# Block boundaries on all tokens at once: two chunks project the unnormed input and are scaled afterwards

## The chip, the cores and the metric

The kernel runs on one core of a Trainium2 chip. The time is device microseconds of one execution of the whole program, inputs in device memory at its start and the output there at its end. A profiled execution also gives a trace: every instruction of TensorE (PE, and PEld for its weight loads), VectorE (DVE), ScalarE (ACT), GpSimd (POOL) and the DMA queues, of which SyncE's (SP) issues nearly all loads.

## What is computed

Two layers on one sequence of 512 tokens with 1024 features, float32. Each layer is a token mixer and a gated MLP, and each of the four sub-layers starts with a norm that is modulated by a conditioning vector:

```python
mod = silu(c) @ ada_w[i] + ada_b[i]
sh1, sc1, g1, sh2, sc2, g2 = split(mod, 6)
h = rms_norm(x, norm_mix[i]) * (1.0 + sc1) + sh1
x = x + g1 * mixer(h)           # layer 0: stick-breaking attention, layer 1: sparse attention with an index
h = rms_norm(x, norm_ffn[i]) * (1.0 + sc2) + sh2
x = x + g2 * conv_ffn(h)        # up-projection, causal conv of width 3, silu(gate) * value, down-projection
```

`rms_norm(x, g)` is `x * rsqrt(mean(x*x) + 1e-6) * g`, with one mean per token. So for one token with the factor r, `h = r * (s * x) + sh`, where s has a value per feature, and for a weight matrix W: `W^T h = r * (W^T (s * x)) + W^T sh`. The right side is what the change uses.

## The kernel before

Everything is kept transposed: features on the 128 partitions, tokens along the row. x is eight tiles of 128 x 512 (`x0` to `x7`), and so is the normed input h. Float32 products are made of three matmuls on a rounded high part and the rest, the low part: high x high, low x high, high x low (`mm3`, lines 249 to 251). Weights come as chunks of 128 x 1024 through six `raw` buffers; ScalarE makes the high part (`whi`, line 209), VectorE the low part (`wlo`, line 217), four buffers of each. A chunk's high part can be made only when PE is done with the chunk four before it. The order of the chunks is a fixed list (`split_order`), and the program says by `split_hi` and `split_lo` where in the queues the next one is split.

A **boundary** is the stretch between two sub-layers: the last output projection (tiles `pt_l`), the residual `x = x + gate * pt_l` (`add_to_x`, line 371, VectorE), the mean of squares (`pt_norm`, `pt_part` on PE with a matrix of ones), the norm factor (a ScalarE seed and three VectorE steps, lines 333 to 335), the normed input (`u` on VectorE, its high part `hhi` on ScalarE, its low part `hlo` on VectorE), and the first four chunks of the next sub-layer (`pt_first`). There are three: attention to MLP of layer 0, MLP to the sparse attention of layer 1, and that to the MLP of layer 1. Each is written by `boundary` in two halves of 256 tokens: the second half's projection covers the first half's norm, the first half of `pt_first` covers the second half's norm, and `second_half` ends the four chunks and hands each result to its consumer. All matmuls of a boundary are thus 256 columns wide. In program order each engine has one queue; the order in the code is the order in the queue, and a scheduler does not reorder inside this part.

Behind a boundary the MLP evacuates each chunk by `evac_up`: ScalarE writes `y` from PSUM (line 999), VectorE adds two shifted products (lines 1000 and 1001), and for a pair `mix` makes silu (ScalarE), the product, and its high (`acthi`, line 233) and low part. Projections use three PSUM banks (`mm`). Behind the second boundary the consumers are the index keys (`kd`, `kl`), the index weights (`kw`) and the query tiles (`qs`, made by `qi_evac`); then come index scores `z`, eight heads of three matmul pairs, between whose heads steps of the next projections are put (`fill`, `drain`).

The modulation is made on VectorE, one dot (line 258) per 128 columns: 24 in the first attention, one or two per head, 56 in the first MLP, one behind each chunk (`ada_steps`).

Of the kernel before, what the change touches and what calls it, by code (L numbers as in the profile page):

```python
# [9 lines left out]
F32 = mybir.dt.float32  # L10
# [9 lines left out]
S = 512  # L20
# [40 lines left out]
def chunk_order():  # L61
# [19 lines left out]
    keys += [("uv",)]  # L81
    return {k: i for i, k in enumerate(keys)}
# [38 lines left out]
def kernel_body(ctx, tc, xT, wst, cst, smalls, crow, ccol, relb, onehot, outT):  # L121
# [28 lines left out]
    sfac = cpool.tile([P, KT], F32, name="sfac")  # L150

# [61 lines left out]
    def split_lo(new=split_tile, engine=dve):  # L213
        while pend_lo:
            k, n, raw, hi = pend_lo.pop(0)
            lo = new("wlo")
            engine.tensor_sub(lo[:, :n], raw[:, :n], hi[:, :n].bitcast(F32))  # L217
            ready[k] = (hi, lo)
# [34 lines left out]
    ada_jobs = [(l, g, f) for l in range(DEPTH) for g in (1, 0, 2, 4, 3, 5) for f in range(KT)][2 * KT:]  # L253
    ada_state = {"i": 0, "cap": 3 * KT}
# [5 lines left out]
    def ada_steps(n):  # L260
        for _ in range(n):
            if ada_state["i"] >= ada_state["cap"]:
                return
            l, g, f = ada_jobs[ada_state["i"]]
            ada_state["i"] += 1
            ada_dot(mod[l][:, g * KT + f:g * KT + f + 1], chunk_raw(("ada", l, g, f)))
# [4 lines left out]
    def ada_until(n):  # L271
        ada_steps(n - ada_state["i"])
# [11 lines left out]
    def square(f, hf):  # L284
        t = npool.tile([P, H2], F32, name="sqt", bufs=5)
        act.activation(t, x[f][:, halves[hf]], AF.Square)
        return t

    def square_add(f, t):
        if f == 0:  # L290
            a = sqs["acc"] = npool.tile([P, H2], F32, name="sqa")
            dve.tensor_copy(a, t)
        else:
            dve.tensor_add(sqs["acc"], sqs["acc"], t)

    def sum_squares(t, start, stop):
        if start:
            sqs["pt"] = ptile([P, H2], "pt_norm", "z")
        pe.matmul(sqs["pt"], lhsT=ones_mean, rhs=t, start=start, stop=stop)

    def quarter_squares(ts, first):

        if first:
            sqs["parts"] = ptile([P, H2], "pt_part", "z")
        for i, t in enumerate(ts):
            pe.matmul(sqs["parts"][32 * i:32 * i + 32], lhsT=ones_mean[:, :32], rhs=t, start=first, stop=not first)

    def quarters_out():
        t = sqs["sum"] = npool.tile([P, H2], F32, name="sqt", bufs=5)
        act.activation(t, sqs["parts"], AF.Copy, scale=D / 32)  # L310
# [1391 lines left out]
```

## Time and profile before

| | |
|---|---|
| median of three runs | 1275.79 us (1274.8 to 1276.78) |
| the profiled execution | 1274.89 us, span 1272.8 us |
| PE busy | 1258.4 us, 99% |
| VectorE, ScalarE busy | 909.3 us (71%), 601.4 us (47%) |
| granted PE clock | 1.00 |
| first, second, third boundary, from the first `pt_l` matmul to the first matmul behind the `pt_first` group | 50.56, 50.94, 50.85 us |

The span is what the trace covers. The page's lists give busy time per engine; a timeline row gives the start, the duration, engine, line and operation, output and inputs, and in brackets the idle time before it with what ended it. A matmul's duration is longer than its distance to the next one, since matmuls are pipelined. A row of a window gives its ends and length, then the busy time (and instructions) of PE, PEld, VectorE, ScalarE and GpSimd, the granted clock, the DMA engines' share and GB/s.

### The profile page before, as it was taken

What the parts mean: (1) busy time and instruction counts of PE and PEld (TensorE: products, weight loads), DVE (VectorE), ACT (ScalarE), POOL (GpSimd) and SP (SyncE); (2) the same over time, 40 slices, a digit from 0 to 9 for tenths busy, and PEclk for the clock granted to TensorE, in tenths of its full rate; (3) what the DMA queues carried; (4) which work ended last, traced back from release to release, by engine and by line L of the source; (5) the groups of instructions that cost most, each with busy time, mean ns of one, the idle gap of its engine ahead of it and who ended that gap; (6) DMA issues with size and microseconds to landing.
All of it is one profiled execution on the core that took longest, in us unless ns stands there. A gap on an engine that the chain in (4) does not pass through costs nothing.

```text
span 1272.8 us, 17764 instructions
## 1 busy us (share of the span) xinstructions
PE 1258.4 (99%) x6774; PEld 1050.5 (83%) x6774; DVE 909.3 (71%) x1543; ACT 601.4 (47%) x1067; POOL 123.9 (10%) x129
## 2 busy tenths in 40 slices
PE   8999999999999999999999999999999999999998
PEld 6988787898888888888897788778988888888887
DVE  5889998778777877885778876567766456456653
ACT  6477666454323323442456357775553334334430
POOL 0000000000000000000002357773000000000000
PEclk9999999999999999999999999999999999999999
DMA  9644434323575575655222211142222322423231
GB/s 372 227 132 134 144 128 139 120 67 128 199 254 185 178 241 191 191 182 157 85 67 67 100 50 51 53 147 68 83 91 74 121 91 75 128 84 100 75 91 67
DMA packets 49893, 163.41 MB, mean 128 GB/s; under 512 B 5728, under 2 KB 7008, under 8 KB 49808
## 3 DMA queue, kind: packets, MB, share of 16 engines
q1 hardware_dynamic: 49376, 161.49, 38.7%
q8 instruction: 53, 0.87, 0.3%
q10 hardware_dynamic: 432, 0.79, 0.2%
q14 instruction: 32, 0.26, 0.1%
HBM read 160.12 MB, written 2.14 MB: 127 GB/s over the span
## 4 chain that ended last, share of the span: by engine, by line
PE 89%; DVE 6%; ACT 2%; DMA 2%; issue 1%; POOL 1%; SPq 0%; DVEq 0%; ACTq 0%
PE pt_u L249 11%; PE pt_u L250 11%; PE pt_u L251 11%; PE pt_d L250 5%; PE pt_d L249 5%; PE pt_d L251 5%; PE pt_first L249 2%; PE pt_first L251 2%; PE pt_first L250 2%; PE pt_q L249 2%; PE pt_q L251 2%; PE pt_q L250 2%; PE pt_l L250 2%; PE pt_l L249 2%; PE pt_l L251 2%; PE pt_qk L249 1%
## 5 line engine op out<-in xcount | busy, mean ns | idle before, releaser
L209 ACT ACTIVATE whi<-raw 128x1024 fp32r<-128x1024 f32 (+1 forms) x206 | 205.3, 1003 | 116.3 <-PE pt_d L251 88.2
L249 PE MATMUL pt_u<-hhi,whi 128*128 128x512 f32 x640 | 249.2, 389 | 0.0
L250 PE MATMUL pt_u<-hhi,wlo 128*128 128x512 f32 x640 | 249.0, 389 | 0.0
L251 PE MATMUL pt_u<-hlo,whi 128*128 128x512 f32 x640 | 249.0, 389 | 0.0
L217 DVE TENSOR_TENSOR wlo<-raw,whi 128x1024 fp32r<-128x1024 f32 (+1 forms) x186 | 214.0, 1152 | 14.1 <-ACT whi L209 13.2
L999 ACT ACTIVATE y<-pt_u,sm 128x512 f32<-128x512 f32 x80 | 62.2, 777 | 188.0 <-PE pt_u L251 188.0
L249 PEld LDWEIGHTS pt_u<-hhi,whi 128*128 128x128 f32 x640 | 120.1, 188 | 26.0 <-issue 1.1
L251 PEld LDWEIGHTS pt_u<-hlo,whi 128*128 128x128 f32 x640 | 120.1, 188 | 24.9
L250 PEld LDWEIGHTS pt_u<-hhi,wlo 128*128 128x128 f32 x640 | 120.2, 188 | 24.7
L1000 DVE SCALAR_TENSOR_TENSOR y<-pt_u,sm,y 128x511 f32<-128x511 f32 x80 | 59.9, 749 | 96.6 <-ACT y L999 96.4
L249 PE MATMUL pt_d<-acthi,whi 128*128 128x512 f32 x288 | 112.0, 389 | 0.0
L250 PE MATMUL pt_d<-acthi,wlo 128*128 128x512 f32 x288 | 112.0, 389 | 0.0
L251 PE MATMUL pt_d<-actlo,whi 128*128 128x512 f32 x288 | 112.0, 389 | 0.0
L258 DVE SCALAR_TENSOR_TENSOR raw<-raw,cond 128x1024 f32<-128x1024 f32 x88 | 106.6, 1217 | 4.7 <-DMA raw<-wst 4.7
L371 DVE SCALAR_TENSOR_TENSOR x<-pt_d,mod,x 128x512 f32<-128x512 f32 x48 | 36.0, 750 | 72.8 <-PE pt_d L251 72.8
L233 ACT ACTIVATE acthi<-y 128x512 fp32r<-128x512 f32 x44 | 27.8, 632 | 105.8 <-DVE y L1018 105.8
L249 PE MATMUL pt_first<-hhi,whi 128*128 128x256 f32 (+1 forms) x224 | 68.3, 305 | 0.0
L250 PE MATMUL pt_first<-hhi,wlo 128*128 128x256 f32 (+1 forms) x224 | 67.1, 299 | 0.8 <-DVE wlo L217 0.8
L251 PE MATMUL pt_first<-hlo,whi 128*128 128x256 f32 (+1 forms) x224 | 66.9, 299 | 0.0
L249 PEld LDWEIGHTS pt_d<-acthi,whi 128*128 128x128 f32 x288 | 54.1, 188 | 11.3
L251 PEld LDWEIGHTS pt_d<-actlo,whi 128*128 128x128 f32 x288 | 54.1, 188 | 11.2
L250 PEld LDWEIGHTS pt_d<-acthi,wlo 128*128 128x128 f32 x288 | 54.1, 188 | 11.2
(253 smaller groups left out, 2655.6 us busy)
## 6 DMA issues: line engine op xcount, KB each, us to landing
raw<-wst SPq DMA_DIRECT2D x250, 512.0 KB, 3.7
raw<-wst SPq DMA_DIRECT2D x48, 384.0 KB, 3.0
th<-rb SPq DMA_DIRECT2D x16, 256.0 KB, 3.4
ada<-wst SPq DMA_DIRECT2D x4, 512.0 KB, 6.3
outT<-x SPq DMA_DIRECT2D x6, 256.0 KB, 2.0
x<-xT SPq DMA_DIRECT2D x5, 256.0 KB, 5.1
x<-xT ACTq DMA_DIRECT2D x3, 256.0 KB, 4.0
cond<-crow SPq DMA_DIRECT2D x1, 512.0 KB, 10.7
```

The costliest lines, as they stand in the source:

```text
L209: act.activation(hi[:, :n], raw[:, :n], AF.Copy)
L217: engine.tensor_sub(lo[:, :n], raw[:, :n], hi[:, :n].bitcast(F32))
L233: act.activation(hi, src, AF.Copy)
L249: pe.matmul(out, lhsT=whi, rhs=ahi, start=start, stop=False)
L250: pe.matmul(out, lhsT=wlo, rhs=ahi, start=False, stop=False)
L251: pe.matmul(out, lhsT=whi, rhs=alo, start=False, stop=stop)
L258: dve.scalar_tensor_tensor(raw, raw, 1.0, cond, op0=OP.mult, op1=OP.mult, accum_out=dst)
L371: dve.scalar_tensor_tensor(x[f][:, c], pt, mod[l][:, g * KT + f:g * KT + f + 1], x[f][:, c], op0=OP.mult, op1=OP.add)
L999: act.activation(y, pt, AF.Identity, scale=cw[2], bias=sm[:, b + S_CB + c:b + S_CB + c + 1])
L1000: dve.scalar_tensor_tensor(y[:, 1:], pt[:, :S - 1], cw[1], y[:, 1:], op0=OP.mult, op1=OP.add)
```

## The change

`boundary` works on all 512 tokens. It projects all of `pt_l` with full-width matmuls, 512 columns. Right behind each residual tile ScalarE makes its square and the rounded `x * s` (`xs`, tiles that `place` takes from buffers free at that moment), VectorE the low part of `x * s`. The first two of the four chunks project `xs`, without the norm. Meanwhile squares are added up on VectorE and PE makes one 512-wide sum behind the third k of these two chunks; then come the norm factor and the normed input, 512 wide, and the other two chunks on it. The first two results are multiplied by the token's factor (`rescale`, VectorE) and get `W^T sh` as a bias per row (`bcol`, ScalarE). `second_half` is gone: consumers take the four results at the end.

`bcol` is made by VectorE dots of a new weight layout (`bt` chunks) with the shift as a row. The shift is a column of `mod`; it is written to device memory and read back as a row on all partitions, four jobs later. This job stands in the list of modulation dots: one in the first attention, two in the first MLP. The list's first groups are reordered, two heads of the attention take a job more, and the first MLP starts its dots one pair of chunks later.

In the sparse attention `kl`'s second half is copied by ScalarE, five fill steps of the fourth query chunk stand ahead of the index scores, and value tiles are 512 wide instead of two of 256.

```diff
-    ada_jobs = [(l, g, f) for l in range(DEPTH) for g in (1, 0, 2, 4, 3, 5) for f in range(KT)][2 * KT:]
-    ada_state = {"i": 0, "cap": 3 * KT}
+    ada_jobs = [(0, g, f) for g in (2, 3, 4) for f in range(KT)]
+    for at, what in ((19, "col"), (23, "row")):
+        ada_jobs.insert(at, ("bias", 0, what))
...
+            nc.sync.dma_start(shifts[n], mod[l][:, g * KT:(g + 1) * KT])
+        else:
+            ov = shifts[n][0:1, 0:1]
+            row = raws.tile([P, D], F32, name="shrow", tag="raw")
+            nc.sync.dma_start(row, bass.AP(tensor=ov.tensor, offset=ov.offset, ap=[[0, P], [1, D]]))
+            for i in range(2):
+                raw = chunk_raw(("bt", n, i))
+                dve.scalar_tensor_tensor(raw, raw, 1.0, row, op0=OP.mult, op1=OP.mult,
+                                         accum_out=bcol[:, 2 * n + i:2 * n + i + 1])
...
-        ops0 = norm_ops(nl, sh, 0)
-        pend = []
-        for m in range(KT):
-            if m == 1:
-                sum_squares(sqs["acc"], True, False)
-                sum_squares(prev, False, True)
-                norm_seed(0)
-            if m == 5:
-                quarter_squares(pend[:4], True)
-            pend.append(out_tile(1, m))
...
+        goals = {0: last[2], 1: last[3], 2: first[0], 4: first[1], 6: first[2]}
...
+            add_to_x(l, gate, m, begun.pop(m))
+            square(m)
+            xs[m] = place(m)
+            act.activation(xs[m][0], x[m], AF.Copy, scale=sfac[:, m:m + 1])
+            if m > 1:
+                square_add(m - 1)
+            if m == KT - 1:
+                square_add(m)
+            if m:
+                scaled_lo(m - 1)
+            split_lo()
+            if m in goals:
+                while pos["i"] <= order.index(goals[m]):
+                    split_hi()
...
+        def rescale(i):
+
+            v = npool.tile([P, S], F32, name="v", tag="sqt", bufs=2)
+            dve.tensor_mul(v, pts[i], rstd["r"])
+            act.activation(v, v, AF.Identity, bias=bcol[:, 2 * n + i:2 * n + i + 1])
+            vs.append(v)
...
+            first_steps((0, 1), xs, k)
+            if k == 2:
+                sum_squares()
+                norm_seed()
+                norm_newton()
+        cs += [chunk(k, 0) for k in first[2:]]
+        for k in range(KT + 1):
+            if k < KT:
+                norm_hi(nl, sh, k)
+            if k:
+                norm_lo(nl, sh, k - 1)
+                first_steps((2, 3), hs, k - 1)
+            if k in (4, 6):
+                split_hi()
+            if k == 6:
+                rescale(0)
+        split_lo(n=1)
+        rescale(1)
+        return pts, vs
...
-        for i in range(4):
-            project(pts[i][:, halves[1]], cs[i], hcur["h"], halves[1])
-            if i in ahead:
-                split_hi()
-            finish(i, pts[i])
-            split_lo()
...
-                    if l == 0:
+                    if l == 0 and j >= 3:
                         ada_steps(1)
...
-                    dve.tensor_sub(kl[64:], pt[64:], kd[64:].bitcast(F32))
...
+                act.activation(kl[64:], kl[64:], AF.Copy)
...
+                ptq = ptile([P, S], "pt_qi", "mm")
+                fill = project_steps(ptq, chunk(("qi", 3), 0))
+                drain(fill, 5)
```

Three places in the queues. VectorE in the first boundary's last projection; `pt_l` is the projected tile, `sqa` the sum of squares, `xkd` and `xkz` low parts of the scaled x, `nt` and `ln` the norm factor. Before:

```order
L371 SCALAR_TENSOR_TENSOR x_94<-pt_l,mod_87,x_94 128x256
L294 TENSOR_TENSOR sqa<-sqa,sqt 128x256
L371 SCALAR_TENSOR_TENSOR x_95<-pt_l,mod_87,x_95 128x256
L294 TENSOR_TENSOR sqa<-sqa,sqt 128x256
L371 SCALAR_TENSOR_TENSOR x_96<-pt_l,mod_87,x_96 128x256
L294 TENSOR_TENSOR sqa<-sqa,sqt 128x256
```

Now:

```order
L371 SCALAR_TENSOR_TENSOR x_97<-pt_l,mod_87,x_97 128x512
L322 TENSOR_TENSOR sqa<-sqa,sqt 128x512
L409 SCALAR_TENSOR_TENSOR xkd_2663<-x_96,sfac,xkd_2662 128x512
L371 SCALAR_TENSOR_TENSOR x_98<-pt_l,mod_87,x_98 128x512
L322 TENSOR_TENSOR sqa<-sqa,sqt 128x512 x2
L409 SCALAR_TENSOR_TENSOR xkz_2686<-x_97,sfac,xkz_2685 128x512
L220 TENSOR_TENSOR wlo<-raw,whi 128x1024
L409 SCALAR_TENSOR_TENSOR xkz_2711<-x_98,sfac,xkz_2710 128x512
L220 TENSOR_TENSOR wlo<-raw,whi 128x1024
L348 TENSOR_TENSOR nt<-ln 128x512
```

A tile has three operations instead of two, of double width, and two weights' low parts stand ahead of the norm factor.

PE in the first two chunks of the first boundary, as it is now:

```order
L254 MATMUL pt_first<-xolo,whi 128x512
L252 MATMUL pt_first<-xohi,whi 128x512
L253 MATMUL pt_first<-xohi,wlo 128x512
L254 MATMUL pt_first<-xolo,whi 128x512
L326 MATMUL pt_norm<-sqa,ones_mean 128x512
L252 MATMUL pt_first<-xohi,whi 128x512
```

The one sum of squares stands between the third and the fourth k; before, there were three sums and two groups of quarter sums per boundary.

ScalarE behind the first boundary; `v` is a rescaled chunk, `y` a chunk's first conv product, `acthi` the high part of the gated product, `whi` a weight's. Before:

```order
L209 ACTIVATE whi<-raw 128x1024
L999 ACTIVATE y_3035<-pt_first,sm 128x512
L386 ACT_TABLE_LOAD
L386 ACTIVATE ecols<-ecols 128x1
L209 ACTIVATE whi<-raw 128x1024
L999 ACTIVATE y_3070<-pt_first,sm 128x512
L1015 ACTIVATE y_3035<-y_3035 128x512
L233 ACTIVATE acthi<-y_3070 128x512
L209 ACTIVATE whi<-raw 128x1024
```

Now:

```order
L455 ACTIVATE v<-v,bcol 128x512
L386 ACT_TABLE_LOAD
L386 ACTIVATE ecols<-ecols 128x1
L991 ACTIVATE y_2886<-v,sm 128x512
L991 ACTIVATE y_2892<-v,sm 128x512
L1007 ACTIVATE y_2886<-y_2886 128x512
L236 ACTIVATE acthi<-y_2892 128x512
L211 ACTIVATE whi<-raw 128x1024
L991 ACTIVATE y_2906<-pt_first,sm 128x512
```

The first `y` now stands behind both rescaled chunks and the table load, and the high part of the next MLP chunk behind `acthi`.

More of the change, by code (lines that the diff above doesn't have):

```diff
@@ L81, in chunk_order @@
     keys += [("uv",)]
+    keys += [("bt", n, i) for n in range(3) for i in range(2)]
     return {k: i for i, k in enumerate(keys)}
@@ L260, in ada_steps @@
     def ada_steps(n):
-        for _ in range(n):
-            if ada_state["i"] >= ada_state["cap"]:
-                return
+        while n and ada_state["i"] < ada_state["cap"]:
             l, g, f = ada_jobs[ada_state["i"]]
             ada_state["i"] += 1
+            if l == "bias":
+                bias_job(g, f)
+                n -= f == "row"
+                continue
+            n -= 1
             ada_dot(mod[l][:, g * KT + f:g * KT + f + 1], chunk_raw(("ada", l, g, f)))
@@ L282, in kernel_body, with square, square_add, sum_squares @@
     sqs = {}
[L284 to L310, printed above, removed]
+    def square(f):
+        t = npool.tile([P, S], F32, name="sqa", tag="u", bufs=3) if f == 0 else \
+            npool.tile([P, S], F32, name="sqt", bufs=2)
+        act.activation(t, x[f], AF.Square)
+        sqs[f] = t
+    def square_add(f):
+        dve.tensor_add(sqs[0], sqs[0], sqs.pop(f))
+    def sum_squares():
+        sqs["pt"] = ptile([P, S], "pt_norm", "z")
+        pe.matmul(sqs["pt"], lhsT=ones_mean, rhs=sqs.pop(0), start=True, stop=True)
     hcur = {}
@@ L386, in warm, with boundary @@
         act.activation(spare, eps_c, func)
-    def boundary(last, O, l, gate, nxt, first):
+    def boundary(n, last, O, l, gate, nxt, first, place):
         cks = [chunk(k, 0) for k in last[:2]]
-        unsplit = lambda: pos["i"] <= order.index(last[3])
         nl, gcol, sh, sc = nxt
@@ L1324, in dsa_layer @@
                 O = []
[L1325 to L1327 removed]
+                uvc = [npool.tile([P, S], F32, name="uvc", tag="sqt", bufs=2) for i in range(2)]
+                for i in range(2):
+                    nc.sync.dma_start(uvc[i], wst[CH["uv",], :, i * S:(i + 1) * S])
                 heads = {}
@@ L1584, in dsa_layer, with place @@
                         follow(engine)
-                first = boundary([("do", 1, m) for m in range(4)], O[4:], l, 2, (l, S_NF, 3, 4), up_first(l))
+                def place(f):
+                    return [pp.tile([P, S], F32R, name="x" + t, tag=t, bufs=QRING) for t in ("qh", "ql")]
+                first = boundary(2, [("do", 1, m) for m in range(4)], O[4:], l, 2, (l, S_NF, 3, 4), up_first(l), place)
         return first, man
```

239 lines of the change are left out of this document (106 added, 133 removed).

## Prediction

> **What bounds the kernel now.** I read the page's first part, then its chain that ended last, then the busy time of each engine by stage, with the three boundaries as windows of their own, and last the timelines inside them.
>
> ```profile
> PE 1258.4 (99%) x6774; PEld 1050.5 (83%) x6774; DVE 909.3 (71%) x1543; ACT 601.4 (47%) x1067; POOL 123.9 (10%) x129
> PE 89%; DVE 6%; ACT 2%; DMA 2%; issue 1%; POOL 1%; SPq 0%; DVEq 0%; ACTq 0%
> 239.96:290.52 50.56, 49.59 (x408) 47.84 (x407) 36.86 (x76) 28.32 (x52) 0.00 (x0) 1.00 0.23 74
> 607.79:658.73 50.94, 49.90 (x407) 47.95 (x406) 37.55 (x78) 27.85 (x52) 1.75 (x6) 1.00 0.25 80
> 880.80:931.65 50.85, 49.91 (x408) 47.96 (x407) 39.20 (x78) 28.35 (x52) 2.15 (x1) 1.00 0.26 84
> ```
>
> TensorE (PE) is the bound: 99% of the span, 89% of the chain, at granted clock 1.00. A window row gives the length, then busy time of PE, PEld, DVE, ACT, POOL. The three windows are the boundaries, each from its first `pt_l` matmul to the first matmul behind its `pt_first` group: 50.56, 50.94 and 50.85 us. PE idles 1 us in each, VectorE 12 to 14 us, ScalarE 22 us. Only PE's instructions and its waits can move the time, but a busy PE is not one at its best rate; that is read from start to start:
>
> ```profile
> 271.80 0.28 PE L249 MATMUL pt_first<-hhi,whi 128*128 128x256 f32 x1
> 271.92 0.28 PE L250 MATMUL pt_first<-hhi,wlo 128*128 128x256 f32 x1
> ...
> 300.07 0.39 PE L249 MATMUL pt_u<-hhi,whi 128*128 128x512 f32 x1
> ...
> 300.75 0.39 PE L249 MATMUL pt_u<-hhi,whi 128*128 128x512 f32 x1
> 253.12 0.86 PE pt_norm L299 x4
> ```
>
> Half-width matmuls start every 0.120 us, full-width ones every 0.227 us (three in 0.68). So two halves cost 0.240.
>
> **PE's own work.** Each boundary has 384 half-width matmuls (96 products twice in `pt_l`, 96 twice in `pt_first`): 384 x 0.120 = 46.1 us. What is left of 50.56 is 4.5 us: the sums of squares in four pieces, and 1 us of waiting for the last squares. After the change there are 192 full-width ones, 192 x 0.2265 = 43.5, and one 512-wide sum, two passes, which I put at what four half-width passes take, 0.86. That is 44.4 us. Saved: 6.2, 6.5 and 6.5 us, 19.2 together, if nobody makes PE wait.
>
> The Trainium skill, "TensorE: Matmul & The Clock Gate", section "Back-to-back issue gap", speaks against most of the merging: a warm matmul costs its columns at 2.4 GHz plus 2.5 ns, so joining two saves 2.5 ns, an estimate of 0.5 us per boundary instead of 2.5. The trace disagrees: the pair above costs 13 ns more than the whole, so the measured spacing stands.
>
> **VectorE inside a boundary.** It now does all tokens' scaling twice: once unnormed for two chunks, once normed for two. Rates when it is queued:
>
> ```profile
> 222.69 0.69 DVE L927 TENSOR_TENSOR olo<-av,ohi 128x512 fp32r<-128x512 f32 x1
> 223.29 1.41 DVE L371 SCALAR_TENSOR_TENSOR x<-pt_o,mod,x 128x512 f32<-128x512 f32 x2
> 224.61 0.42 DVE L880 TENSOR_TENSOR_SCAN mz<-mz,diag 128x128 f32<-128x128 f32 x1
> 283.84 0.75 DVE L1000 SCALAR_TENSOR_TENSOR y<-pt_first,sm,y 128x511 f32<-128x511 f32 x1 [3.81 <-ACT y L999]
> 284.63 0.75 DVE L1001 SCALAR_TENSOR_TENSOR y<-pt_first,sm,y 128x510 f32<-128x510 f32 x1
> 285.29 1.21 DVE L217 TENSOR_TENSOR wlo<-raw,whi 128x1024 fp32r<-128x1024 f32 x1
> 259.06 1.23 DVE L217 TENSOR_TENSOR wlo<-raw,whi 128x1024 fp32r<-128x1024 f32 x1 [0.28 <-ACT whi L209]
> 260.20 0.48 DVE L342 SCALAR_TENSOR_TENSOR u<-ln,sfac,x 128x256 f32<-128x256 f32 x1
> 687.69 0.59 ACT L1091 ACTIVATE qh<-pt_q 128x512 fp32r<-128x512 f32 x1
> 688.17 0.60 ACT L1092 ACTIVATE q2g<-pt_q 128x512 f32<-128x512 f32 x1
> 268.19 1.04 ACT L209 ACTIVATE whi<-raw 128x1024 fp32r<-128x1024 f32 x1
> 269.14 0.36 ACT L310 ACTIVATE sqt<-pt_part 128x256 f32<-128x256 f32 x1
> ```
>
> From start to start: a 512-wide TENSOR_TENSOR 0.60, a 512-wide SCALAR_TENSOR_TENSOR 0.66 (0.79 when the next needs its result), a weight's low part 1.14, a 512-wide ACT copy 0.48, a weight's high part 0.95. The `pt_l` stage gives VectorE per tile `add_to_x` 0.66, the square's add 0.60 and the scaled input's low part 0.66, so 1.92, against 12 x 0.2265 = 2.72 us of PE. Three or four weights' low parts (five or six at the second and third boundary, whose last two chunks are not split yet) add 1.14 each. Counted from the first `pt_l` matmul, tile 0 is there at 4.9 (21 matmuls; the first two tiles interleave). Walking the queue in its printed order I get x7 at 22, the last add at 24.2, against PE's sum of squares at 21.7 + 18 x 0.2265 = 25.8: no wait, with 1.6 us to spare (1.2 at the other two). The low parts of tile 7 and of the fourth chunk end at 27.7; then come Newton's three steps, to 30.0. From there each k takes two 0.66 operations, 1.32, against 1.36 for PE's six matmuls: the first normed low part is ready at 32.4, PE wants it at 34, the last at 42.3 against 43.5. So PE never waits inside, by a margin of about 1 us; its bounds are 0 and the price in the last rival. Nearer to the boundary's end PE's spacing is a little wider in the trace:
>
> ```profile
> 290.52 0.40 PE L249 MATMUL pt_u<-hhi,whi 128*128 128x512 f32 x1
> ...
> 291.22 0.40 PE L249 MATMUL pt_u<-hhi,whi 128*128 128x512 f32 x1
> ```
>
> 0.233 instead of 0.227. I take 0.3 us per boundary for it (0 to 1.2, as if all 192 ran so): 0.9 in all.
>
> **What is late next: the first MLP chunks (boundaries one and three).** Before, the four chunks' results came 2.9 us apart (24 x 0.120) and were evacuated between. Now all four end almost together, with VectorE and ScalarE behind.
>
> ```profile
> 283.82 1.28 ACT L386 ACT_TABLE_LOAD   x1
> 285.12 0.20 ACT L386 ACTIVATE ecols<-ecols 128x1 f32<-128x1 f32 x1
> ...
> 290.82 1.43 ACT L999 ACTIVATE y<-pt_first,sm 128x512 f32<-128x512 f32 x2
> ```
>
> Low part of chunk `up 2,0` to 43.4, second rescale `v` to 43.9, its bias on ScalarE to 44.7, then table load and warm-up, 1.4, to 46.1, `y` 0.67 (two in 1.43), the two conv steps to 48.3, low part `up 2,1` to 49.5 (PE wants it at 50.1: in time), the second conv to 51, multiply 51.7, `acthi` 52.3. Only behind that, in ScalarE's queue, stands the high part of `up 3,0`, to 53.3; then `y` of the third chunk 54, its conv 55.4, and only then, in VectorE's queue, the low part, to 56.7. PE reaches that chunk at 44.4 + 48 x 0.2265 = 55.3 and wants the low part with its second matmul: 1.2 to 1.5 us of waiting, partly for the PSUM bank that the conv empties. `up 3,1` follows by the same round trip, 0.8 us late. From `up 4` on VectorE has 4.7 us less to do per pair of chunks than PE and the delay is gone. So 2.3 us at the first boundary, 2.7 at the third (two low parts more): 5.0. Bounds: 0 and 8.
>
> The Trainium skill, "ScalarE: Activation LUTs", section "What ACT_TABLE_LOAD costs", has 1.28 us plus a drain of 1.38. By it the chain would be 1.4 us longer at each of the two, and the forecast 2.8 us higher. The rows show the next ACT instruction 0.02 us behind the load, on an engine that had just ended its work; I keep 1.3.
>
> **The second boundary ends in the index scores.**
>
> ```profile
> 658.73:682.57 23.84, 23.66 (x117) 19.71 (x116) 19.34 (x32) 14.69 (x29) 0.00 (x0) 1.00 0.15 45
> 667.87 0.28 PE L1252 MATMUL z<-kd,qs 128*128 128x256 f32 x1
> ...
> 663.58 1.39 DVE L1174 TENSOR_TENSOR qs<-pt_first,qs 64x512 fp32r<-64x512 f32 x2 [0.26 <-ACT qs L1170]
> 665.00 2.07 DVE L1257 SCALAR_TENSOR_TENSOR work<-rl,wT,work 128x256 f32<-128x256 f32 x4
> ```
>
> Before, `kd`, `kl` and two query tiles were made while PE still projected; now the second rescaled chunk is ready at 44.9 and all follows: two `kd` copies, `kl`, its copy, two query copies, a low part, to 48.9. PE is covered by five of the eight fill steps, 15 x 0.23 = 3.5, and four transposes: 44.4 to 48.2. It waits 0.7. But those five steps are then missing between the scores of heads 0 to 2, where VectorE has two query pairs, a weight's low part and `wT` first (to 52.1) and then 1.6 us per head plus 1.4 for the next query pair: to 58.3. With two PSUM banks and three `rl` buffers PE can be about 0.7 ahead of that, so head 3 starts at 57.6. Before, it started at 667.87 - 607.79 = 60.1. Of 6.5 us gained 2.5 are left; 4.0 are lost (bounds 0 and 6.5: later heads have their fill as before).
>
> **Elsewhere.** Two modulation dots more (the shift row's) in the attention, where VectorE is the second bound, and a broadcast row with its two weight chunks through the six `raw` buffers; four more in the first MLP.
>
> ```profile
> 100.00:239.00 139.00, 138.68 (x823) 112.54 (x824) 127.89 (x194) 89.79 (x190) 0.00 (x0) 1.00 0.42 139
> 340.00:605.00 265.00, 265.00 (x1171) 219.43 (x1170) 200.09 (x282) 92.53 (x121) 0.00 (x0) 1.00 0.62 199
> L258 DVE SCALAR_TENSOR_TENSOR raw<-raw,cond 128x1024 f32<-128x1024 f32 x88 | 106.6, 1217 | 4.7 <-DMA raw<-wst 4.7
> ```
>
> 1.2 us each. The attention has 11 idle VectorE microseconds in 139, the MLP 65 in 265: four dots there cost nothing (0 to 5 if the cover were gone). The attention's two I put at 0.3 (0 to 2.4). The row's DMA stands on SP's queue behind the column's, written four jobs earlier, some 25 us at that stage's pace; SP should find it landed; if not, the weight loads queued behind it on SP wait, and PE for those. The boundaries load the same chunks as before. The `vals` copy as one instruction and the second table of values in two loads take a little off ScalarE: nothing on the path.
>
> **Sum.** 19.2 - 0.9 - 5.0 - 4.0 - 0.3 = 9.0 us. The profiled execution took 1274.89, 2.09 around its span of 1272.8, and lies 0.9 under the median of the runs; 1265.9 against it, 1266.8 against the median. I say 1266.
>
> **Rivals.**
> *The whole gain.* The queues behind a boundary catch up sooner than my walk says. For: the chain to `up 3,0` has some fifteen links, each lateness there is the small difference of two sums of 55 us, and VectorE idles 12 to 14 us of each boundary before. Against: the links are one behind another in the printed order. Then 1274.9 - 18 = 1257, or 1261 with the index stage's loss alone. Chance 0.2.
> *A longer round trip.* Every late chunk of the MLP waits for ScalarE's `acthi` and VectorE's conv; if the table switch holds ScalarE 1.4 us longer, or `up 4` is late too, boundaries one and three lose 2 to 3 us more each: 1270 to 1272. Against: the 0.02 us behind the load. The Trainium skill's drain, above, would lead here. Chance 0.12.
> *VectorE becomes the bound in the boundary, slower.* If its operations don't overlap there because each needs its neighbour's result, the spacing is 0.79 and 0.72, not 0.66 and 0.60. A tile costs 2.3, two operations per k 1.58, more than PE's 1.36. The last normed low part comes at 45 in the first boundary and 47.5 in the others, 1 and 3.5 us late, and the chunks behind it about 2.5 later still: 5 of 6.2 us lost, then 8.5 and 10 of 6.5. Time 1274.9 + 4 = 1279. It decides from a spacing of about 0.77. Against: the printed order puts another tile's work between dependent operations. Chance 0.07; in between, with everything just eaten up, 0.05 for no change. (0.2% is about what a measurement of this kernel tells from none.)
>
> **Chances and range.** Forecast 0.56, whole gain 0.2, longer round trip 0.12, no change 0.05, slower 0.07. Faster 0.88, same 0.05, slower 0.07. The range reaches to the first two rivals: 1258 to 1272.
>
> **What would show it.** Right: the three windows from `pt_l` to the end of `pt_first` near 44.5 us; no PE wait of any size for `sqa`, `xolo` or `hlo`; PE waits of 1 us for `wlo` or for the conv step a few microseconds behind boundaries one and three; index heads 1 and 2 without PE fill. Wrong: windows of 47 or more with waits on `hlo`; a PE wait for an `a` of the attention or for a shift row; `up 3` starting on time.

## The result and the profile after

The changed kernel takes 1267.26 us (median of four, 1266.47 to 1268.48), the kernel before 1275.62 beside it: ratio 0.9935, 95% interval 0.9917 to 0.9952. The profiled execution took 1266.66 us, its span is 1264.7. The prediction was 1266, faster.

The page of the changed kernel, busy time and the chain that ended last (shares of the span by engine):

```profile
PE 1246.9 (99%) x6138; PEld 1016.6 (80%) x6138; DVE 928.2 (73%) x1503; ACT 608.5 (48%) x1035; POOL 124.1 (10%) x129
PE 80%; DVE 12%; ACT 4%; issue 3%; DMA 2%; POOL 1%; SPq 0%; DVEq 0%; ACTq 0%
```

PE has 636 matmuls and 11.5 us less, and VectorE's share of the chain has doubled, from 6 to 12%: PE now meets VectorE at more places. The windows of the changed kernel, cut at the boundaries (ends, length, busy PE, PEld, VectorE, ScalarE, GpSimd, granted clock, DMA share, GB/s):

```profile
241.64:286.74 45.10, 45.10 (x197) 36.53 (x195) 37.34 (x53) 26.19 (x38) 0.00 (x0) 1.00 0.19 61
286.74:605.86 319.12, 318.02 (x1398) 261.16 (x1396) 248.98 (x349) 116.76 (x154) 0.00 (x0) 1.00 0.62 201
605.86:650.29 44.43, 44.43 (x195) 36.42 (x194) 38.34 (x55) 25.75 (x37) 2.18 (x6) 1.00 0.25 81
650.29:674.50 24.21, 21.94 (x97) 17.39 (x96) 18.99 (x31) 16.83 (x32) 0.00 (x0) 0.93 0.20 66
876.89:921.32 44.43, 44.43 (x195) 36.42 (x194) 39.42 (x55) 25.85 (x37) 2.14 (x1) 1.00 0.28 83
921.32:1264.70 343.38, 338.58 (x1513) 280.41 (x1511) 191.32 (x233) 120.70 (x157) 0.00 (x0) 1.00 0.30 92
```

The three boundaries are 44.4 to 45.1 us long and PE is busy in all of each. What was gained there is partly given back in between. In the index stage (fourth row) PE idles 2.3 us, and the granted clock is 0.93, which no row of before had. Stage by stage, each from the first matmul of the kind named to the next:

| stage | before | change | difference | forecast |
|---|---|---|---|---|
| start to the attention's first `tr` | 71.61 | 71.34 | -0.3 | 0 |
| attention, to the first `pt_l` | 168.35 | 170.30 | +1.95 | +0.3 |
| boundary 1 | 50.56 | 45.10 | -5.5 | -5.9 |
| first MLP | 317.27 | 319.12 | +1.85 | +2.3 |
| boundary 2 | 50.94 | 44.43 | -6.5 | -6.2 |
| index and sparse attention | 222.07 | 226.60 | +4.5 | +4.0 |
| boundary 3 | 50.85 | 44.43 | -6.4 | -6.2 |
| second MLP, to the end | 341.15 | 343.38 | +2.2 | +2.7 |
| span | 1272.80 | 1264.70 | -8.1 | -9.0 |

These stages repeat within 0.1 us from trace to trace where the code is the same (one second MLP was 0.4 us shorter); only the start does not, 71.3 to 73.6 us in the 13 traces of the change and its variants, though nothing there was edited, and, as will be seen, the index stage. So experiments are read by the stages first and by the medians second.

The waits of PE in the changed kernel (in all us, how often, the longest); the rows for `nm`, `kn` and the start are as before and left out:

```profile
PE tr L880 <- DVE a L865: 2.5, 3, 1.4
PE z L1247 <- ACT rl L1251: 2.3, 3, 1.1
PE pt_u L253 <- DVE wlo L220: 2.2, 4, 0.6
...
PE pt_u L252 <- DVE y L993: 0.4, 1, 0.4
```

There is no wait for `xs`, for the sum of squares or for `hlo`. The first row was 0.9 us before, the second 0.2, the others were not there. The chain behind the first boundary, out of the timeline of all engines of the changed kernel:

```profile
285.83 0.72 ACT L455 ACTIVATE v<-v,bcol 128x512 f32<-128x512 f32 x1 [2.62 <-DVE v L454]
286.57 1.28 ACT L386 ACT_TABLE_LOAD   x1
287.97 1.51 ACT L991 ACTIVATE y<-v,sm 128x512 f32<-128x512 f32 x2
293.75 0.63 ACT L236 ACTIVATE acthi<-y 128x512 fp32r<-128x512 f32 x1 [2.68 <-DVE y L1010]
294.29 1.04 ACT L211 ACTIVATE whi<-raw 128x1024 fp32r<-128x1024 f32 x1
297.48 1.21 DVE L220 TENSOR_TENSOR wlo<-raw,whi 128x1024 fp32r<-128x1024 f32 x1
298.75 0.50 PE L253 MATMUL pt_u<-hhi,wlo 128*128 128x512 f32 x1 [0.57 <-DVE wlo L220]
```

These are the prediction's links: rescale, table, `y`, `acthi`, and only then the high part of `up 3,0`, whose low part PE waits for. A wait of 0.57 us costs more than 0.57: the matmul ahead starts 1.04 us earlier instead of 0.23, and the one behind follows after 0.34. Two such stops, at `up 3,0` and `up 3,1`, are the 1.85 us of the first MLP. In the second MLP the first matmul of `up 3,0` also waits 0.42 us for the conv step that empties its PSUM bank, the last row of the list of waits.

And the attention (VectorE's and PE's timelines of the changed kernel):

```profile
99.88 1.22 DVE L286 SCALAR_TENSOR_TENSOR raw<-raw,cond 128x1024 f32<-128x1024 f32 x1
102.36 0.69 DVE L865 TENSOR_TENSOR a<-a,mz 128x512 f32<-128x512 f32 x1
103.10 0.33 PE L880 MATMUL tr<-cons,a 128*128 128x128 f32 x1 [1.35 <-DVE a L865]
```

The extra dot of head 2 stands ahead of that head's last scan; PE, which waited 0.24 us for this `a` before, now waits 1.35. The same at head 8: 0.53, none before. These two are 1.6 of the 1.95 us that the attention lost.

### The profile page after: what moved, and what is told of

Read it like the earlier page. It is cut to its first block, busy times and chain, and to the rows that moved or that the text cites. A ratio compares the mean times of both kernels' runs of the same rounds, so it can differ in the third digit from the quotient of the medians.

```text
span 1264.7 us, 16443 instructions
## 1 busy us (share of the span) xinstructions
PE 1246.9 (99%) x6138; PEld 1016.6 (80%) x6138; DVE 928.2 (73%) x1503; ACT 608.5 (48%) x1035; POOL 124.1 (10%) x129
## 4 chain that ended last, share of the span: by engine, by line
PE 80%; DVE 12%; ACT 4%; issue 3%; DMA 2%; POOL 1%; SPq 0%; DVEq 0%; ACTq 0%
PE pt_u L253 11%; PE pt_u L252 11%; PE pt_u L254 11%; PE pt_d L253 5%; PE pt_d L252 5%; PE pt_d L254 5%; DVE wlo L220 2%; PE pt_q L252 2%; PE pt_q L254 2%; PE pt_q L253 2%; PE pt_l L252 1%; PE pt_l L254 1%; PE pt_l L253 1%; PE av L902 1%; PE av L1458 1%
## 5 line engine op out<-in xcount | busy, mean ns | idle before, releaser
L993 DVE SCALAR_TENSOR_TENSOR y<-pt_u,sm,y 128x510 f32<-128x510 f32 x80 | 59.9, 749 | 2.8
L1412 DVE CUSTOM_DVE_ANT_0 L<-z,L,cols 128x128 f32<-128x128 f32 (+1 forms) x64 | 34.8, 547 | 31.7 <-PE tr L1427 20.0
```

Of the source, the lines that this page charges most:

```text
L993: dve.scalar_tensor_tensor(y[:, 2:], pt[:, :S - 2], cw[0], y[:, 2:], op0=OP.mult, op1=OP.add)
L1412: dve.tensor_tensor_reduce(L, z[:, :ns], L, rq[:, c:c + 1], -USED, op0=OP.add, op1=OP.min, accum_out=nm[:, j:j + 1])
```

## The experiments

Theory: the boundaries gain what the spacing says, because the unnormed input covers the norm; what is given back are separate losses behind them, each with a cause of its own (place of the dots, order of ScalarE's queue, missing fill in the index scores). Rivals: VectorE's total load, the weights' transfers, or a ScalarE drain is behind the losses; or the gain is that of width alone. All edits are against the changed kernel.

### The changed kernel again

> The changed kernel once more, as the yardstick of the three runs beside it. If the profiled execution of the change was typical, the time is 1266.5 to 1268.5 us, PE waits 2.3 us for the rl tiles of the index heads 1 and 2, and the four microseconds behind them run at a granted clock near 0.57 again. If that clock drop was an accident of one execution, it is gone or stands elsewhere, and the span varies by up to 1.7 us from execution to execution for that reason.

1267.87 us (ratio 0.9936, 0.9923 to 0.9948). All stages as in the table within 0.1 us but the index stage, 226.28. PE's waits in it are the same 2.3 us, and the clock drop is there again, a little earlier (0.92 and 0.68 in the same two windows as below). So neither is an accident of one execution.

### The clock in the index stage

The changed kernel, the two windows around the end of head 2, and PE's timeline there:

```profile
658.00:663.00 5.00, 2.73 (x11) 1.46 (x11) 4.92 (x9) 2.95 (x7) 0.00 (x0) 1.00 0.18 69
663.00:667.00 4.00, 4.00 (x13) 3.30 (x13) 3.71 (x7) 2.41 (x5) 0.00 (x0) 0.57 0.01 2
```

```profile
662.10 0.50 PE L1247 MATMUL z<-kd,qs 128*128 128x512 f32 x1 [1.09 <-ACT rl L1251]
...
665.14 0.63 PE L253 MATMUL pt_lat<-hhi,wlo 128*128 128x512 f32 x1
665.57 0.63 PE L254 MATMUL pt_lat<-hlo,whi 128*128 128x512 f32 x1
...
667.07 0.40 PE L253 MATMUL pt_lat<-hhi,wlo 128*128 128x512 f32 x1
667.30 0.40 PE L254 MATMUL pt_lat<-hlo,whi 128*128 128x512 f32 x1
```

PE has work for 2.73 of 5 us; then, without a wait, matmuls start every 0.43 instead of 0.23 us for 3.4 us. The experiment gives PE something to do in those waits:

```diff
+                BUSY = {(1, 3): 4, (2, 2): 1, (2, 3): 4}
...
+                        for _ in range(BUSY.get((h, j), 0)):
+                            pe.matmul(busy, lhsT=kd[:, :P], rhs=kd, start=True, stop=True)
```

> Nine matmuls of 512 columns (0.2265 us each, 2.04 us in all) are added where PE waits for rl in the index heads 1 and 2: four ahead of the last score of head 1, one and four ahead of the second and last of head 2; their result is not used. Theory (clock): the 0.57 granted clock from 663 to 667 us comes from PE idling 2.3 us of the 5 us ahead; with PE kept busy the clock stays at 1.00, the matmuls there start every 0.23 instead of 0.42 us, and the time falls by 1.3 to 1.9 us although PE has more to do. Rival (something else slows those matmuls, a port or a transfer): they stay slow, and the time is the same or up to 0.5 us longer.

```profile
659.30:664.30 5.00, 4.78 (x19) 2.80 (x18) 4.79 (x10) 3.11 (x7) 0.00 (x0) 1.00 0.23 87
664.30:668.30 4.00, 3.96 (x19) 3.10 (x19) 3.71 (x8) 3.34 (x7) 0.00 (x0) 1.00 0.01 2
```

The clock stays at 1.00 and the stage takes 225.35 us in place of 226.28 and 226.60, with 2 us of matmuls more. The median is 1266.21 (0.9929, 0.9916 to 0.9941), 1.7 us below the changed kernel beside it, within the intervals. The mean clock of each timed execution tells the rest. Change, nine executions: 1.000 once (1265.20 us), 0.999 three times (1266.47, 1266.59, 1267.87), 0.998 once (1266.66), 0.997 four times (1267.87, 1268.40, 1268.42, 1268.48). With the fill: 1.000 four times, 0.999 once. So the idling costs its own time and then about another 0.9 to 1.3 us by the clock, in most executions.

### The order of the queues behind the boundary

Two edits of the same chain, separately. The table load ahead of the second rescaled chunk's bias:

```diff
         split_lo(n=1)
+        if n != 1:
+            warm(AF.Silu)
         rescale(1)
...
             pts, vs = first
-            warm(AF.Silu)
```

> The load of the silu table (and its warm-up) is put ahead of the second rescaled chunk's bias in ScalarE's queue, behind the last hhi, where ScalarE idles 2.6 us; at the first and third boundary only. Theory (the chain of links to chunk up 3,0 sets the wait): y of the first chunk starts 1.4 us earlier, and with it everything up to the low part of up 3,0, which was 0.57 us late and cost 1.1 us of PE; the low part of up 3,1 was 0.55 us late and cost 0.7. Both waits go at both boundaries: 3.5 to 4 us less. Rival (the weights' transfer or the PSUM bank sets it): the low part or the bank is as late as before, 0 to 1 us less. Rival (a drain of ScalarE at each table load that the rows do not show): the load costs more where it stands now, hhi or the bias comes later, and less than 2 us are won.

```profile
283.39 1.28 ACT L386 ACT_TABLE_LOAD   x1
284.68 0.20 ACT L386 ACTIVATE ecols<-ecols 128x1 f32<-128x1 f32 x1
285.99 0.72 ACT L455 ACTIVATE v<-v,bcol 128x512 f32<-128x512 f32 x1 [1.10 <-DVE v L454]
286.62 1.51 ACT L993 ACTIVATE y<-v,sm 128x512 f32<-128x512 f32 x2
```

The load now lies in ScalarE's idle time, the bias starts when VectorE's `v` is there, and `y` follows at once. The MLPs take 317.60 and 341.80 us: 1.5 and 1.6 of the 1.85 and 2.2 lost are back, 3.1 where 3.5 to 4 were expected. 1263.78 us (0.9909, 0.9896 to 0.9923). In the profiled execution the index scores idled the same 2.3 us, yet the clock stayed at 1.00 and the stage took 225.34: the same waits do not bring the clock down every time (the last section has what the traces say of it).

The high part of `up 3,0` ahead of `acthi`, its low part ahead of `actlo`, the table where it was:

```diff
                 if i == 0:
                     split_lo()
+                    split_hi()
                 if i % 2:
-                    mix(i // 2, *ys[-2:])
+                    mix(i // 2, *ys[-2:], lo=i == 1)
                 if i:
                     split_lo()
-                if i == 1:
-                    split_hi()
```

(With `lo`, `mix` calls `split_lo` between the product and `acthi`.)

> Behind the first and third boundary the high part of chunk up 3,0 is made right behind the first chunk's y on ScalarE, instead of behind acthi, and its low part behind the first product on VectorE, ahead of actlo; the table load stays where it is. Theory (order of the queue): by the rows the low part then ends at about 295 instead of 298.7 us, 2.5 us before PE wants it; the wait at up 3,0 goes (1.1 and 1.5 us), up 3,1 gains the 0.5 us that the third chunk's conv starts earlier: 2.5 to 3.5 us less in all. Rival (transfer or buffer: the raw tile or the whi buffer is free only then): the high part waits where it stands now and holds up y behind it: no change or slower.

```profile
289.63 1.04 ACT L211 ACTIVATE whi<-raw 128x1024 fp32r<-128x1024 f32 x1
294.59 1.22 DVE L220 TENSOR_TENSOR wlo<-raw,whi 128x1024 fp32r<-128x1024 f32 x1
298.12 0.39 PE L253 MATMUL pt_u<-hhi,wlo 128*128 128x512 f32 x1
```

The low part ends at 295.8, PE uses it at 298.12 without a wait. MLPs: 317.34 and 341.53, so 1.8 and 1.85 us won. 1264.04 (0.9908, 0.9891 to 0.9924). Either edit takes most of the same loss away, and neither touches the weights' transfers, so these were not behind it; it was the length of one chain. The PSUM bank is a link of that chain: the 0.42 us of waiting for the conv step are gone in both. A drain of ScalarE is not tested by these edits; the rows speak against it, since the load starts 0.02 us behind the bias, and the next instruction at most 0.02 us behind the load.

### The place of the dots

```diff
-                ada_steps(2 if i % 2 or i in (2, 8) else 1)
+                ada_steps(2 if i % 2 or i in (10, 12) else 1)
```

> The two heads that take a modulation job more are 10 and 12 in place of 2 and 8; the work is the same. Theory (place): PE's waits for an `a` behind heads 2 and 8, 1.1 us more than before at 103 us and 0.53 us new at 169 us, come from the second dot standing ahead of the scan there; with the dots at heads where VectorE has idle time they go, the first pt_l matmul starts at 240.0 instead of 241.64 us, and the time falls by 1.5 us. Rival (load): VectorE is so full in the whole attention that 2.4 us more of work cost the same wherever they stand: no change, the waits turn up behind heads 10 and 12. Rival (transfer): the row of the shift or its two weight chunks hold up SP's queue: no change either, with a DMA wait on VectorE or PE late in the attention.

```profile
102.88 0.33 PE L880 MATMUL tr<-cons,a 128*128 128x128 f32 x1 [0.20 <-DVE a L865]
212.18 0.33 PE L851 MATMUL z<-kz,qs 128*128 128x128 f32 x1 [0.94 <-DVE kz L796]
```

The attention takes 169.21 us, 1.1 less. The waits for `a` are back to 0.8, but head 12 was a bad choice too: its dot delays `kz`, 0.94 us. Head 10 costs nothing. 1266.26 (0.9928, 0.9914 to 0.9941). So it is the place, and the rival of total load falls; it falls for good below, where the one job more that there is to do stands at head 10 and the attention takes 168.4 us, the time of before. The shift's row and its two weight chunks are still loaded there, so their transfers cost nothing either.

### Width alone

72 of the 96 products of `pt_l` and the 48 of the first two chunks in halves of 256 columns (the loop over halves outside the loop over k):

```diff
-                out_steps(m, range(4))
+                for c in halves:
+                    out_steps(m, range(4), c)
...
-        for k in range(KT):
-            first_steps((0, 1), xs, k)
-            if k == 2:
+        for c in halves:
+            for k in range(KT):
+                first_steps((0, 1), xs, k, c)
+                if k == 5 and c == halves[0]:
```

> In the changed boundary 72 of the 96 products of pt_l and all 48 of the first two chunks are made in two halves of 256 columns again (120 full-width matmuls become 240 half-width ones per boundary); nothing else differs. Theory (spacing): two halves cost 0.240 us where one costs 0.2265, so each window from the first pt_l to the end of pt_first grows by 1.6 us, to 46.0 (46.7 the first); VectorE's queues behind are late by less of it, so PE's waits for wlo behind boundaries one and three shrink by up to 0.8 each: 3 to 5 us slower in all. Rival (a joined pair saves 2.5 ns only, the rule of the Trainium skill, TensorE: Matmul & The Clock Gate, Back-to-back issue gap): windows grow by 0.3 us, 1 us slower in all at most.

```profile
242.20:288.24 46.04, 46.04 (x316) 42.64 (x315) 37.42 (x53) 26.42 (x38) 0.00 (x0) 1.00 0.18 60
607.12:653.10 45.98, 45.98 (x315) 42.67 (x314) 38.52 (x55) 26.61 (x38) 2.12 (x6) 1.00 0.26 79
877.69:923.68 45.99, 45.99 (x316) 42.68 (x315) 39.59 (x55) 26.70 (x38) 2.13 (x1) 1.00 0.28 83
```

+0.94, +1.55 and +1.56 us for 120 pairs: 13 ns each in the second and third boundary, 8 in the first, where full-width matmuls are a little slower. The formula of the Trainium skill (TensorE: Matmul & The Clock Gate, Back-to-back issue gap) gives 2.5 ns, an estimate of 0.3 us; the measured number decides. That section of the Trainium skill calls it the gap of isolated matmuls and says that in a stream with a weight load to each, as here, both set the spacing. The prediction and this run's rival took the formula without that reservation. In all only 1268.89 (0.995, 0.9935 to 0.9965), below the 3 to 5 us expected: the windows lose 4.05, but the MLPs win 1.0 back and the index stage 2.0 (224.59, waits of 1.7 us, clock 1.00 in this execution). The windows decide here: by the total alone the rival's 1 us would have looked right.

### All tokens at once, without the unnormed input

The first two chunks project `hs` as well, behind the norm (the loop over the first two chunks stands inside the norm's loop, the other two chunks follow it; `xs` and its low parts are gone, `rescale` only copies; the shift's dots stay, unused):

```diff
-            xs[m] = place(m)
-            act.activation(xs[m][0], x[m], AF.Copy, scale=sfac[:, m:m + 1])
...
-            first_steps((0, 1), xs, k)
-            if k == 2:
-                sum_squares()
...
+                first_steps((0, 1), hs, k - 1)
```

> All tokens at once stay, but the first two chunks project the normed input too: no scaled unnormed input, no rescaling (the shift's dots are still made, their result is not used). Theory (cover): PE has nothing between its last pt_l and the first hlo, about 7 us less the sum: the last square is added at 24, sum to 25, seed and Newton's steps to 28, the first u, hhi, hlo to 30, so that each window is about 51.5 us, no better than the 50.6 to 50.9 of before; such an idle stretch also costs clock, 1.7 us or more per boundary. With the losses behind the boundaries about 1285 to 1293 us, slower than before. So the gain of the change is the cover, and full width by itself is a loss. Rival (VectorE's relief pays): the stage of pt_l has 0.66 us less per tile, norm and input come earlier, windows of 46 to 48, and 1270 to 1276 us.

The windows of this kernel, and PE's timeline behind the first boundary's sum:

```profile
243.91:299.25 55.34, 48.30 (x196) 38.37 (x195) 36.45 (x50) 25.93 (x36) 0.00 (x0) 0.91 0.21 66
616.49:671.33 54.84, 47.72 (x195) 38.20 (x194) 35.38 (x49) 25.05 (x35) 2.27 (x6) 0.91 0.26 84
895.46:949.10 53.64, 46.61 (x195) 37.38 (x194) 38.78 (x52) 26.18 (x36) 2.13 (x1) 0.94 0.28 88
```

```profile
268.66 1.12 PE L326 MATMUL pt_norm<-sqa,ones_mean 128*128 128x512 f32 x2 [2.29 <-DVE sqa L322]
274.52 0.80 PE L252 MATMUL pt_first<-hhi,whi 128*128 128x512 f32 x1 [4.74 <-ACT hhi L357]
275.97 0.63 PE L252 MATMUL pt_first<-hhi,whi 128*128 128x512 f32 x1
```

1291.77 us (1.0127, 1.0112 to 1.0142): slower than before. PE idles 2.3 and 4.7 us, the 7 that were expected, and the clock is at half for 6 us behind it (0.43 us from start to start), dearer than the 1.7 us put in. So the change's gain needs the cover by the unnormed chunks. Full width without it is a loss: the three boundaries alone are 11.5 us longer than before, and of the 16 us in all some 2 are the attention's, whose extra dots are still made. The MLPs, 317.24 and 341.00, lose nothing here: no rescaled chunk, no late chain.

### How much VectorE could be late

```diff
                 norm_seed()
+                for _ in range(4):
+                    dve.tensor_tensor(x[0], x[0], x[0], op=OP.max)
                 norm_newton()
```

> Four operations of VectorE, 512 wide and without effect, stand ahead of Newton's steps in each boundary: each needs the one ahead of it, so some 2.8 us in all. Theory (the slack inside is 1.8 to 2.1 us, and what VectorE is late behind the boundary is paid in full by PE): PE waits 0.7 to 0.9 us for hhi and hlo in each window (45.2 to 45.3 us, 45.9 the first), and the chains behind come 2 us later against PE: 2 us more at up 3,0 in both MLPs and 1.5 to 2 in the index stage: 7 to 9 us slower in all. Rival (the queues behind have room, VectorE idles a quarter of the time): only the waits inside, 2 to 3 us in all.

```profile
242.11:288.57 46.46, 46.01 (x196) 36.30 (x195) 39.60 (x57) 25.29 (x36) 0.00 (x0) 1.00 0.17 54
609.16:655.48 46.32, 45.35 (x196) 36.12 (x195) 40.50 (x58) 25.42 (x36) 2.27 (x6) 1.00 0.24 78
```

The four operations took 2.87 us; the windows grew by 1.4, 1.9 and 1.85, so 1.0 to 1.5 us were slack, less than the 1.8 to 2.1 expected here and near the prediction's "about 1". The stages behind grew by 1.5, 0.7 and 0.9. In all 8.2 us; 1276.28 us, no different from before (1.0005, 0.9995 to 1.0014). In the changed kernel VectorE is 73% busy, and yet 2.9 us more of it per boundary eat the whole change: 0.95 us of time for each microsecond of VectorE.

### More fill for the index scores

`lat` from head 1, dq 0 from head 4, dq 1 from head 7:

```diff
                     if h == 0:
                         qi_evac(2, pts[3])
-                    if h == 2:
                         drain(fill)
-                        qi_evac(3, ptq)
                         ptlat = ptile([P, S], "pt_lat", "mm")
...
+                    if h == 2:
+                        qi_evac(3, ptq)
-                    if h in (3, 6):
+                    if h in (2, 4):
                         prefetch(pos["i"])
-                    if h == 5:
+                    if h in (3, 6):
                         drain(fill)
```

> In the index scores the steps of the next projection start one head or more earlier: lat from head 1 instead of 3, dq 0 from head 4 instead of 6, dq 1 from head 7; the same work in another order. Theory (PE lacks fill in heads 1 and 2, and its idling there costs clock): waits of 2.3 us and the half-clock stretch (1.7 us) go; from the end of pt_first to the end of the scores' stage about 4 us are won, less what the earlier splits of dq 0 and dq 1 on VectorE cost in heads 2 and 4: 2.5 to 4 us less. Rival (VectorE bounds this stage, 1.6 us per head and the query tiles): PE's fill only moves the wait to heads 6 and 7 or into the first projections behind: 0 to 1 us less.

226.13 us against 226.28 and 226.60: hardly anything (1266.88; 0.9934, 0.9919 to 0.9949). The wait for `rl` fell to 0.6 us and the clock stayed at 1.00 there, but PE then waited 0.5 and 1.9 us for the parts of dq 2, and the stretch of half clock came behind these instead:

```profile
685.99:689.40 3.41, 3.19 (x8) 2.52 (x9) 2.92 (x12) 0.79 (x3) 2.50 (x2) 0.50 0.47 154
```

(The next run was expected on the reading that this stretch had gone; it had moved.) Take off the 0.9 to 1.3 us that such a stretch cost above, and the stage is at about 225, an estimate, as good as the change's own at full clock, 225.34: the rival is right here. The next run splits dq 2 in head 6 (`h in (2, 4, 6)`):

> As the run that starts the index stage's fill one head or more earlier (e7_fill), and the split of dq 2 goes into the end of head 6, on ScalarE and VectorE, where there it stood behind all scores with its low part on GpSimd (2.36 us). Theory (in e7_fill PE's wait of 2.3 us for rl and the half-clock stretch did go, and a new wait took their place: 0.5 us for the high and 1.9 us for the low part of dq 2): without it the stage from the end of pt_first to the third boundary, 226.6 us in the changed kernel and 226.1 in e7_fill, falls to 223.5 to 224.5, and the time by 2 to 3 us. Rival (VectorE bounds the stage): its 1.2 us in head 6 come back as a wait of PE for rl or for the first projections: 225.5 to 226.

```profile
690.79 1.25 PE L1213 MATMUL pt_kT<-cons,kn 128*128 128x128 f32 x4 [4.01 <-DVE kn L1206]
...
693.12 0.63 PE L252 MATMUL pt_q<-hhi,whi 128*128 128x512 f32 x1
```

Worse: 228.82 us for the stage, 1269.09 in all (0.9944, 0.9928 to 0.9961). PE reaches `pt_kT` too early and waits 4.0 us for VectorE's `kn`, and then has half clock for 6 us. At full clock these 6 us would have been 3, an estimate, and the stage 225.8: the rival's 225.5 to 226. In these two runs PE's work, moved, only moved the wait. That VectorE bounds the stage fits both, but no run gave VectorE less to do there, so it is argued and not shown.

### Together

First all of it with the index fill of the last run and one extra job, at head 10:

> All that helped, together: one extra modulation job, at head 10 (25 jobs are all there are); the silu table ahead of the second rescaled chunk's bias; up 3,0 split behind the first chunk's y; the index fill of e8_ahead. Theory (four separate losses behind the boundaries, each with a cause of its own): attention 168.4 to 168.6 us in place of 170.3, MLPs 317.3 and 341.2 to 341.5 in place of 319.1 and 343.4, sparse attention's stage 223.5 to 224.5 in place of 226.6: 8 us less than the change, 1258 to 1260 us. Rival (the losses share a cause, so that mending one shifts the wait to the next stage, as PE comes earlier to the same VectorE): less than 5 us, 1262 to 1265.

1262.52 us (0.9895, 0.9881 to 0.991). Attention 168.41 and MLPs 317.23 and 340.99 are as expected, the index and sparse attention 228.30, 4 us above: the fill does here what it did alone, and the total lies where the rival had it, though not for the rival's reason. Then without that fill, with the nine matmuls instead:

> What helped, without the moved index fill, which only carried PE's wait from the scores to pt_kT (4.0 us) and left the clock at 0.5 behind it: the extra modulation job at head 10 alone, the silu table ahead of the second rescaled chunk's bias, up 3,0 split behind the first chunk's y, and the nine unused matmuls in index heads 1 and 2. Theory (the stages' losses are separate and add up): attention 168.4 us, MLPs 317.2 and 341.0, the stage from the end of pt_first to the third boundary 225.3, windows 45.1, 44.4, 44.4 as before: 1257.5 us of span at an average start, 6.5 to 7.5 us less than the change, 1259.5 to 1261 us. Rival (PE, earlier at the second boundary, meets transfers or VectorE less far): a stage grows by over 0.5 us against the runs that changed it alone, and the time is over 1262.

1261.24 us (0.9884, 0.9868 to 0.9901): attention 168.44, MLPs 317.24 and 340.99, index and sparse attention 225.32, each as in the run that had it alone. This beats both kernels, the change by some 6 us. The losses were separate. Left is the index stage, 3.25 us longer than before.

## Why the prediction was right

**PE's own work: right.** 44.4 us per boundary was forecast, 44.43 measured in two, 45.10 in the first. The wider spacing, put at 0.3 us in each, was there in the first alone (0.231 us for its first 34 us) and cost 0.7. Without the cover (the run on the normed input) the same boundaries take 54 to 55 us.

**VectorE inside: right.** The walk through its queue came within 0.6 us at each link of the first boundary: last square added 24.7 (24.2 forecast), PE's sum 26.4 (25.8), Newton 30.3 (30.0), last low part 42.4 (42.3), second rescale 44.1 (43.9). The slack of about 1 us is what the delay showed. The third rival, VectorE as the bound, would have needed 0.77 from start to start; it ran at 0.66.

**The first MLP chunks: right mechanism, a little too dear.** 5.0 us were forecast, 4.1 measured (1.85 and 2.2). The links came where the walk had them (`acthi` 52.7 for 52.3, low part of `up 3,0` 57.0 for 56.7); both stops, at `up 3,0` and `up 3,1`, are there, and two edits of the chain each take nearly all of it away. The second rival, a ScalarE drain behind the table load (the Trainium skill, ScalarE: Activation LUTs, What ACT_TABLE_LOAD costs), does not show: the load of 1.28 us starts 0.02 us behind the instruction ahead of it, the next follows within 0.02 us, and moving the load away won 1.5 us, the load and its warm-up.

**The index stage: 4.0 forecast, 4.5 measured, but not by the forecast's parts.** The first score of head 3 was to start at 57.6 us from the boundary's first matmul; it started at 56.9 (662.73 - 605.86). So missing fill cost 3.3 us, not 4.0. The rest, 1.2, is the clock, which the prediction did not think of. Two errors of opposite sign: that 4.0 came so near is luck.

**The attention's extra dots: the term that was mis-sized.** "The attention's two I put at 0.3 (0 to 2.4)"; measured 1.95, inside the bound, and a wait for an `a`, which the prediction had named as a sign of being wrong, did come. The step set two dots against VectorE's idle time over the whole stage (11 us in 139). But head 2 had none at its place: the trace of before already showed PE waiting there for `a`, and an extra 1.15 us ahead of that scan was paid in full. Moving the job gives it back. In the sum the 1.65 us missing here and 0.5 in the index stage are met by 0.9 too much for the MLPs and 0.3 of the start, so that the total, 9.0 against 8.1, is nearer than its terms; that is luck too.

**Why the first rival did not come.** The whole gain (1257 us) would have needed the queues behind the boundaries to catch up, and they do not. With the dots moved, the table load and the chain reordered and nine unused matmuls to keep up the clock it nearly does, 1261.24 us, and what is missing is the index stage.

## What to carry over

Extra work on an engine that is not the bound is priced where it stands, by the wait behind it there, and not by the stage's idle share: 1.2 us of VectorE was free at head 10 and cost 1.1 us of PE at head 2. When a stage of the bounding engine gets shorter, walk the queues behind it as links with their order, since the cheapest mends here were places in an in-order queue (a table load in idle time, a weight's split two links earlier). And where short waits of TensorE crowd together, look at the granted clock of the next microseconds too.

## What had not been expected of the hardware

**TensorE's clock fell after short waits.** Three waits of 2.3 us in all within 5 us, the longest 1.1, were followed by 3.4 us at half clock in four of the five profiled executions that had these very waits (the change twice, and the kernels with moved dots and with the reordered chain), not in the fifth (moved table load). The half clock starts behind the waits, on matmuls that wait for nothing, so no list of waits shows it. Windows show its ends; three of the changed kernel, then two of the kernel with the moved table load:

```profile
659.98:663.39 3.41, 2.04 (x10) 1.21 (x9) 3.36 (x7) 1.75 (x5) 0.00 (x0) 1.00 0.02 5
663.39:666.80 3.41, 3.41 (x10) 2.79 (x9) 3.12 (x6) 2.02 (x5) 0.00 (x0) 0.50 0.01 2
666.80:670.21 3.41, 3.41 (x18) 2.83 (x17) 2.45 (x4) 2.46 (x5) 0.00 (x0) 1.00 0.00 0
655.76:659.17 3.41, 2.25 (x11) 1.34 (x10) 3.19 (x8) 2.80 (x6) 0.00 (x0) 1.00 0.39 149
659.17:662.58 3.41, 2.32 (x11) 1.52 (x12) 3.38 (x7) 1.96 (x5) 0.00 (x0) 1.00 0.00 0
```

Behind the wait of 4.0 us the clock was at half for 6.8 us, in the normed boundaries for 10.2, 10.2 and 6.8: always one, two or three times 3.41. Within a trace the changes also lie whole steps of 3.413 us apart: the three falls of the normed kernel, at 270.35, 642.40 and 922.29, 109 and 82 steps. So the clock seems to be set by steps that run through the execution whatever the kernel does. In the changed kernel one step holds enough of the waits to leave PE busy for 2.04 of 3.41 us (60%), and the clock falls. In the last two rows, counted back from a fall at the end of their trace (1259.92 us, 176 steps behind 659.17), two steps share the same waits, at 66 and 68%, and the clock stays. It came back behind steps with PE busy for 3.19 us or more, not behind those with 2.68 or less. This is read from traces; no run shifted the waits against the steps. Nor is PE's busy time a clean threshold: behind the 2.03 us of the step from 101.89 us on in the kernel with VectorE's four extra operations the clock stayed.

The Trainium skill (TensorE: Matmul & The Clock Gate, What's actually happening) has a clock that halves after an idle window of some 3.4 us and comes back after a busy one, with windows that run freely. The half clock, the steps of 3.41 us and the return agree with it. That the window must be idle does not: 60% busy was too little.

**Left open.** In the first boundary full-width matmuls start every 0.231 us for 34 us, in the others every 0.227, and half-width ones show no such difference; no run tells why.
